# 384 unused bytes in front of the split weights' buffers of a decoder trunk

## The chip, the cores and the metric

The kernel runs on one NeuronCore of a Trainium2 chip, in float32 and float32r. The metric is the device time of one execution in microseconds (us). TensorE multiplies, ScalarE and VectorE work on elements, GpSimd does a few small operations, and SyncE (SP) issues the weight loads. On-chip memory has 128 partitions; an offset in this text is a byte offset within a partition.

## The reference, cut to what matters

256 tokens of width 2048 go through a feed-forward block, a token mixer and a second feed-forward block:

```python
def _swiglu(h, w_gu, w_down):
    gate, up = jnp.split(h @ w_gu, 2, axis=-1)
    return (jax.nn.silu(gate) * up) @ w_down
...
        x = x + 0.5 * _swiglu(_rmsnorm(x, ffn1_norm[l]), ffn1_w_gu[l], ffn1_w_down[l])
        x = x + _token_mixing(_rmsnorm(x, mix_norm[l]), w_in[l], qk_gain[l], sinks[l], cmp_pos[l], cmp_w1[l],
                              cmp_w2[l], w_branch_a[l], w_branch_b[l], w_branch_c[l], w_out[l])
        x = x + 0.5 * _swiglu(_rmsnorm(x, ffn2_norm[l]), ffn2_w_gu[l], ffn2_w_down[l])
```

The mixer is one wide input projection, three kinds of attention over it, a gated product per branch and an output projection. All weights together are 401 MB, and each is used once, so most of the work is multiplying 256 tokens with a stream of weights.

## The kernel before

**The weight stream.** Every large product goes through `add_chunk` (lines 148 to 179): an output of 256 tokens by at most 512 columns in two PSUM banks, one for each block of 128 tokens (`tb`). The weights come in loads of up to 4 x 128 rows into three buffers `raw`, issued in order by SyncE (line 103). Each load is cut into units of two slices of 128 rows, and each unit is split into two float32r parts: ScalarE copies `raw` to `hi` (line 111), and VectorE takes the rest to `lo` (line 112). There are four buffers `hi` and four `lo`, used in turn; `stream` (lines 127 to 144) splits three to four units ahead of the one that is multiplied.

**The matmuls.** The activations are split in the same way, part 0 and part 1, and are transposed, with features on the partitions. For each slice of 128 rows and each token block there are three matmuls that add up in one bank:

```python
                    PE.matmul(o, lhs(kt, 0, tb), hi[:, k], start=kt == 0, stop=False)
                    PE.matmul(o, lhs(kt, 0, tb), lo[:, k], start=False, stop=False)
                    PE.matmul(o, lhs(kt, 1, tb), hi[:, k], start=False, stop=kt == nkt - 1)
```

The first argument after the output is the stationary operand, a 128 x 128 slice of the activations that an LDWEIGHTS instruction (PEld in the profile) puts into the array. The second is the moving operand, a slice of `hi` or `lo` with up to 512 columns. These are lines 162, 163 and 164. The stationary tile depends on the stage:
- `xT`, the normalised input, in both gate-up products and in the mixer's input projection. The projection has chunks of 384, 420 and 512 columns.
- `ffn1_midt` and `ffn2_midt`, the gated hidden values, in the down products (ffn_midt in the profile);
- `oT`, the attention outputs, in the branch products, and `mT`, their gated sum, in the output projection.

**Other work of TensorE.** Transposes against `ident` of the input (line 219), of the hidden values (line 269), of queries, keys and probabilities (lines 479, 718), the float32 attention products (lines 750 to 859), and the hidden layer of the key compression (line 627), which also takes `hi` and `lo` as moving operands, with 256 columns, and slices of `Xs` with 66 columns as stationary ones. The order on each engine is the order in which the program is written: there is no scheduler.

**Where the tiles lie.** Tiles of the pool `per` stand behind one another in the order of their allocation, each rounded up to 32 bytes:

```python
    x_sb = per.tile([128, 2, D], F32, name="x_sb")
    xT = per.tile([128, KT, 2, T], F32R, name="xT")
    raws = [per.tile([128, LOAD_KT * 512], F32, name=f"raw{i}") for i in range(RAW_BUFS)]
    his = [per.tile([128, SPLIT_KT * 512], F32R, name=f"hi{i}") for i in range(SPLIT_BUFS)]
    los = [per.tile([128, SPLIT_KT * 512], F32R, name=f"lo{i}") for i in range(SPLIT_BUFS)]
    ident = per.tile([128, 128], F32, name="ident")
```

The stages' pools follow behind `per`; those that are opened with `side="right"` grow from the other end. In the built program the offsets modulo 512 bytes are:

| Tiles | modulo 512 before |
|---|---|
| `x_sb`, `xT`, `raw`, `hi`, `lo`, `ident` | 128 |
| `ffn1_midt`, `ffn2_midt`, `oT`, `mT`, and the rows that line 269 transposes (`m`) | 0 |
| `Xs` (right side) | 64; its slices step by 264 bytes |
| `pt` | 192 |

A stationary slice takes 512 bytes of a partition and a slice of `hi` or `lo` with 512 columns 2048 bytes, so every slice of these tiles begins where its tile does, modulo 512. In a chunk of 420 columns the second slice of a unit begins 1680 bytes behind the first, which is 272 modulo 512.

Of the kernel before, what the change touches and what calls it, by code (L numbers as in the profile page):

```python
# [9 lines left out]
F32 = mybir.dt.float32  # L10
# [6 lines left out]
T, D, FF = 256, 2048, 5632  # L17
# [15 lines left out]
class Ring:  # L33
    """Buffers handed out and given back in emission order."""

# [11 lines left out]
def hybrid_trunk_kernel(ctx, tc, x, ffn1_norm, ffn1_w_gu, ffn1_w_down, mix_norm, w_in, qk_gain, sinks, cmp_pos,  # L47
# [13 lines left out]
    xT = per.tile([128, KT, 2, T], F32R, name="xT")  # L61
    raws = [per.tile([128, LOAD_KT * 512], F32, name=f"raw{i}") for i in range(RAW_BUFS)]
    his = [per.tile([128, SPLIT_KT * 512], F32R, name=f"hi{i}") for i in range(SPLIT_BUFS)]
    los = [per.tile([128, SPLIT_KT * 512], F32R, name=f"lo{i}") for i in range(SPLIT_BUFS)]
# [9 lines left out]

# [1 line left out]
    chains = []  # L76
# [15 lines left out]
    loads, subs = [], []  # L92

    def add_load(src, nk, width, parts):
        """src: [128, nk, width] in DRAM; parts: [(k0, nk, mm, before, after)]"""
        li = len(loads)
        loads.append((src, nk, width))
        for k0, n, mm, before, after in parts:
            subs.append((li, k0, n, width, mm, before, after))
# [5 lines left out]
    def emit_split(si, k=None):  # L105
        """split of a unit, or of its k-th slice of 128 rows"""
        li, k0, n, width, *_ = subs[si]
        c = slice(0, n * width) if k is None else slice(k * width, (k + 1) * width)
        raw = raws[li % RAW_BUFS][:, k0 * width:(k0 + n) * width][:, c]
        hi, lo = his[si % SPLIT_BUFS][:, c], los[si % SPLIT_BUFS][:, c]  # L110
        ACT.activation(hi, raw, AF.Copy)  # L111
        DVE.tensor_tensor(lo, raw, hi.bitcast(F32), op=OP.subtract)  # L112
# [35 lines left out]
    def add_chunk(w, rows0, nkt, c0, width, lhs, evac, before=None, between=()):  # L148
        """out[tok, c0:c0+width] = lhs^T @ w[rows0:rows0+128*nkt, c0:c0+width]; lhs(kt, part, tb) -> [128, 128]."""
        bank = main[2 * (chunk_no[0] % 2):][:2]  # L150
        chunk_no[0] += 1
        wv = w[rows0:rows0 + 128 * nkt, c0:c0 + width].rearrange("(k p) c -> p k c", p=128)

        def mm_of(kt0, n):
            def mm(hi, lo):
                ks = [(k, tb) for k in range(n) for tb in range(2)]
                if kt0 + n == nkt:
                    ks.sort(key=lambda a: a[1])
                for k, tb in ks:
                    kt = kt0 + k  # L160
                    o = bank[tb][:, :width]
# [3 lines that stand above are left out]
            return mm  # L165

        step = SPLIT_KT if not loads else LOAD_KT
        for l0 in range(0, nkt, step):
            ln = min(step, nkt - l0)
            parts = []  # L170
            for s0 in range(0, ln, SPLIT_KT):
                sn = min(SPLIT_KT, ln - s0)
                last = l0 + s0 + sn == nkt
                first = l0 + s0 == 0
                parts.append((s0, sn, mm_of(l0 + s0, sn), before if first else None,
                              (lambda: evac(bank)) if last else None))
            add_load(wv[:, l0:l0 + ln], ln, width, parts)
            for args in between[l0 // step:l0 // step + 1]:
                add_load(*args)
# [14 lines left out]

# [1 line left out]
    def x_squares(j):  # L196
# [9 lines left out]
    def x_prep(norm, j):  # L206
        """The norm's share of columns 512j.., and their transposed two-part copy with the gain."""
        g0 = GAIN_ROW[norm]
# [25 lines left out]

# [1 line left out]
    def add_ffn(norm, w_gu, w_down, done):  # L236
# [68 lines left out]

# [1 line left out]
    tabs = {}  # L307
# [8 lines left out]
    def row_cols(r0, r1, c0):  # L316
        """rows [0, r1) as columns, of which [r0, r1) are kept from column c0 on"""
        b = banks.take()
        PE.transpose(b[:, :r1], rows[:r1, :], ident[:r1, :r1])
        DVE.tensor_copy(cols[:, c0:c0 + r1 - r0], b[:, r0:r1])  # L320
        banks.give(b)
# [7 lines left out]

# [1 line left out]
    def build_tables():  # L331
        """Negated key distances, far below zero where a key is masked; constants of the heads' slopes."""
        p = tab_pool
# [63 lines left out]
    def add_mix(done):  # L397
# [36 lines left out]

        # per-head norms, transposes of queries and keys
        def raw_of(bank, width):
# [5 lines left out]
        def normed(bank, qr, c0, nh, const):  # L442
            """heads in qr[:, :, c0:c0+64nh]; bank is free to be written"""
            w = 64 * nh
# [24 lines left out]
        def transposed(jobs, finish):  # L469
            """jobs: (source of tb, evac); two jobs share a bank"""  # L470
            for a in range(0, len(jobs), 2):
# [21 lines left out]
        def q_evac(name, p0, h0, const):  # L493
            """six query heads h0.. to the pairs p0.."""
            def f(bank):
# [30 lines left out]
        def both_halves(dst, src, gain):  # L526
            """dst(g)[0:64] = dst(g)[64:128] = src[64g:64g+64] * gain"""
            for g in range(2):
# [25 lines left out]
        def ckv1_evac(bank):  # L554
            """k_cmp, v_cmp, k_slc"""
            qr = raw_of(bank, 384)
# [27 lines left out]
        def make_x(i):  # L584
            """cmp MLP input of keys (0) or values (1), two-part, on partitions (offset parity, d)"""
            X, Xs = st["X"], st["Xs"]
# [13 lines left out]
        def ckv2_evac(bank):  # L600
            """v_slc, k_win, v_win, gates"""
            for tb in range(2):
# [11 lines left out]
        def cmp_loads(i):  # L614
            """hidden layer of the cmp MLP: two loads, to be set between a chunk's"""
            wv = cmp_w1[0, i].rearrange("(k p) c -> p k c", p=128)
# [74 lines left out]

        # attention
        att = {"S": True, "O": True, "obs": {}}
# [15 lines left out]
        def apply_p(sb, blocks, pv):  # L709
            """blocks: (column of sb, keys); transposes them, then pv(pt, block index)"""  # L710
            while not (banks.free and att["O"] and st["pt"].free):
# [166 lines left out]
        def launcher():  # L878
            """starts attention units at a steady pace"""
            for name, marks, group in units:  # L880
# [15 lines left out]

        # gates, branch products, output projection
        def open_gates():
# [121 lines left out]

# [1 line left out]
    x2 = x[0].rearrange("(t p) d -> p t d", p=128)  # L1022
# [47 lines left out]
    g = gens[0]  # L1070
# [50 lines left out]
```

## Time and profile before

| What | Value |
|---|---|
| median of 3 runs | 2246.64 us (2246.13 to 2247.63) |
| span of the profiled execution | 2244.8 us |
| TensorE busy | 2229.0 us, 99% of the span, 10417 matmuls |
| LDWEIGHTS busy | 1861.9 us, 83% |
| VectorE, ScalarE, GpSimd busy | 54%, 45%, 3% |
| read from HBM | 401.03 MB, 180 GB/s |

The span is one execution under the profiler, from its first to its last instruction; the times are of executions without it. A matmul's duration in a row reaches past the start of the next one, since matmuls overlap in the array. What a matmul costs in a row of many is the distance in time from its start to the next one's start, called a step below.

### The profile page before, as it was taken

The numbers are of one execution on the slowest core, as the hardware profiler recorded it, in microseconds if no ns is written. First come the engines' busy times: TensorE is split into PE (matmuls) and PEld (weight loads), VectorE is DVE, ScalarE is ACT, GpSimd is POOL, SyncE is SP. The second block draws the span as 40 slices with busy tenths as digits, with TensorE's granted clock in tenths as the row PEclk, the third lists the DMA queues.
The fourth block names the chain that finished last, engine by engine and source line by source line (L and its number), as shares of the span: only waits on it lengthen the run. The fifth ranks groups of instructions, "written<-read, shape, count | busy, mean of one in ns | idle before, by whom it ended". The sixth has DMA issues, their size and how long they took to land.

```text
span 2244.8 us, 26058 instructions
## 1 busy us (share of the span) xinstructions
PE 2229.0 (99%) x10417; PEld 1861.9 (83%) x10417; DVE 1210.3 (54%) x1618; ACT 1019.4 (45%) x1368; POOL 67.1 (3%) x83
## 2 busy tenths in 40 slices
PE   8999999999999999999999999999999999999999
PEld 7888888888888999998888888788888888888887
DVE  5755544455555576666555554555555544555553
ACT  5444433444444565555555444454444433444432
POOL 0000000000000121000001110100000000000000
PEclk9999999999999999999999999999999999999999
DMA  7555555555555564333345555555555555555553
GB/s 247 187 188 191 192 184 188 196 193 187 188 187 183 169 214 139 120 120 132 131 151 176 201 182 176 190 180 188 191 193 187 190 189 191 189 188 188 189 205 131
DMA packets 212626, 404.82 MB, mean 180 GB/s; under 512 B 7368, under 2 KB 36632, under 8 KB 212504
## 3 DMA queue, kind: packets, MB, share of 16 engines
q1 hardware_dynamic: 211696, 402.98, 52.9%
q8 instruction: 81, 1.33, 0.2%
q14 instruction: 41, 0.34, 0.0%
q10 hardware_dynamic: 808, 0.17, 0.0%
HBM read 401.03 MB, written 2.10 MB: 180 GB/s over the span
## 4 chain that ended last, share of the span: by engine, by line
PE 97%; DVE 1%; DMA 1%; POOL 0%; ACT 0%; issue 0%; SPq 0%; POOLq 0%; ACTq 0%
PE main L162 31%; PE main L164 30%; PE main L163 30%; PE misc L269 1%; PE misc L718 1%; PE misc L859 1%; PE misc L831 1%; POOL mg L958 0%; DVE lo L112 0%; PE misc L219 0%; PE misc L750 0%; PE misc L856 0%; ACT hi L111 0%; PE misc L832 0%; PE misc L769 0%
## 5 line engine op out<-in xcount | busy, mean ns | idle before, releaser
L112 DVE TENSOR_TENSOR lo<-raw,hi 128x1024 fp32r<-128x1024 f32 (+3 forms) x785 | 938.3, 1198 | 878.3 <-ACT hi L111 873.8
L111 ACT ACTIVATE hi<-raw 128x1024 fp32r<-128x1024 f32 (+3 forms) x785 | 808.1, 1032 | 922.4 <-PE main L164 906.1
L162 PE MATMUL main<-hi,xT 128*128 128x512 f32 (+1 forms) x2176 | 839.6, 386 | 3.1 <-ACT hi L111 3.1
L164 PE MATMUL main<-hi,xT 128*128 128x512 f32 (+1 forms) x2176 | 828.5, 381 | 0.0
L163 PE MATMUL main<-lo,xT 128*128 128x512 f32 (+1 forms) x2176 | 828.1, 381 | 0.1
L162 PEld LDWEIGHTS main<-hi,xT 128*128 128x128 f32 x2176 | 409.7, 188 | 81.7 <-issue 6.6
L164 PEld LDWEIGHTS main<-hi,xT 128*128 128x128 f32 x2176 | 409.0, 188 | 70.8
L163 PEld LDWEIGHTS main<-lo,xT 128*128 128x128 f32 x2176 | 409.3, 188 | 69.4 <-DVE lo L112 0.8
L162 PE MATMUL main<-hi,ffn_midt 128*128 128x512 f32 x704 | 278.4, 395 | 0.0
L164 PE MATMUL main<-hi,ffn_midt 128*128 128x512 f32 x704 | 277.9, 395 | 0.0
L163 PE MATMUL main<-lo,ffn_midt 128*128 128x512 f32 x704 | 277.8, 395 | 0.0
L164 PEld LDWEIGHTS main<-hi,ffn_midt 128*128 128x128 f32 x704 | 132.5, 188 | 31.2
L162 PEld LDWEIGHTS main<-hi,ffn_midt 128*128 128x128 f32 x704 | 132.5, 188 | 31.1
L163 PEld LDWEIGHTS main<-lo,ffn_midt 128*128 128x128 f32 x704 | 132.5, 188 | 30.9
L162 PE MATMUL main<-hi,mT 128*128 128x512 f32 x128 | 50.9, 398 | 0.0
L164 PE MATMUL main<-hi,mT 128*128 128x512 f32 x128 | 50.5, 395 | 0.0
L163 PE MATMUL main<-lo,mT 128*128 128x512 f32 x128 | 50.5, 394 | 0.0
L725 ACT ACTIVATE pt<-misc 128x256 f32<-128x256 f32 (+2 forms) x44 | 21.1, 490 | 58.8 <-PE misc L718 58.8
L190 DVE TENSOR_TENSOR ffn_midt<-misc,ffn_midt 128x512 fp32r<-128x512 f32 x44 | 28.3, 686 | 32.7 <-ACT ffn_midt L189 32.7
L189 ACT ACTIVATE ffn_midt<-misc 128x512 fp32r<-128x512 f32 x44 | 23.9, 596 | 46.4 <-PE misc L269 46.4
L845 ACT ACTIVATE sb<-sb,nm 128x32 f32<-128x32 f32 (+2 forms) x72 | 29.0, 403 | 28.9 <-DVE nm L839 28.9
L252 ACT ACTIVATE ffn_sg<-main,rstd_ffn 128x512 f32<-128x512 f32 x44 | 30.2, 688 | 22.8 <-PE main L164 20.4
(177 smaller groups left out, 1059.6 us busy)
## 6 DMA issues: line engine op xcount, KB each, us to landing
raw<-in_ffn_w_gu_dram SPq DMA_DIRECT2D x172, 1024.0 KB, 4.9
raw<-in_ffn_w_down_dram SPq DMA_DIRECT2D x88, 1024.0 KB, 5.0
raw<-in_w_in_dram SPq DMA_DIRECT2D x48, 1024.0 KB, 4.9
raw<-in_w_in_dram SPq DMA_DIRECT2D x44, 768.0 KB, 4.3
raw<-in_w_out_dram SPq DMA_DIRECT2D x16, 1024.0 KB, 5.0
raw<-in_ffn_w_gu_dram SPq DMA_DIRECT2D x8, 512.0 KB, 6.2
raw<-in_cmp_w_dram SPq DMA_DIRECT2D x4, 1024.0 KB, 5.8
raw<-in_w_branch_b_dram SPq DMA_DIRECT2D x4, 1024.0 KB, 5.0
```

Of the source, the lines that this page charges most:

```text
L111: ACT.activation(hi, raw, AF.Copy)
L112: DVE.tensor_tensor(lo, raw, hi.bitcast(F32), op=OP.subtract)
L162: PE.matmul(o, lhs(kt, 0, tb), hi[:, k], start=kt == 0, stop=False)
L163: PE.matmul(o, lhs(kt, 0, tb), lo[:, k], start=False, stop=False)
L164: PE.matmul(o, lhs(kt, 1, tb), hi[:, k], start=False, stop=kt == nkt - 1)
L189: ACT.activation(dst_hi, src, AF.Copy)
L190: DVE.tensor_tensor(dst_lo, src, dst_hi.bitcast(F32), op=OP.subtract)
L252: ACT.activation(st["sg"][tb], bank[tb], AF.Sigmoid, scale=r)
L269: PE.transpose(bv[:, k, tb * 128:(tb + 1) * 128], m[tb][:, c0:c0 + 128], ident)
L718: PE.transpose(place[i][:n], sb[:, c0:c0 + n], ident)
L831: PE.matmul(S0[:, :32 + nk], q, st["KC"][g][head_rows(h), :32 + nk], start=True, stop=True)
L845: ACT.activation(s, s, AF.Exp, bias=nm[:, 0, i:i + 1], scale=-1.0, accum_out=nm[:, 1, i:i + 1])
```

## The change

A tile of 96 float32 values per partition, 384 bytes, is allocated between `raw` and `hi`; nothing reads or writes it. `hi`, `lo` and every tile behind them on that side stand 384 bytes further: `hi` and `lo` come to 0 modulo 512, `ident` as well, and `ffn1_midt`, `ffn2_midt`, `oT`, `mT` and `m` to 384. `x_sb`, `xT`, `raw` and the tiles on the right side stay where they were.

```diff
@@ -60,6 +60,7 @@
     x_sb = per.tile([128, 2, D], F32, name="x_sb")
     xT = per.tile([128, KT, 2, T], F32R, name="xT")
     raws = [per.tile([128, LOAD_KT * 512], F32, name=f"raw{i}") for i in range(RAW_BUFS)]
+    per.tile([128, 96], F32, name="split_shift")
     his = [per.tile([128, SPLIT_KT * 512], F32R, name=f"hi{i}") for i in range(SPLIT_BUFS)]
     los = [per.tile([128, SPLIT_KT * 512], F32R, name=f"lo{i}") for i in range(SPLIT_BUFS)]
     ident = per.tile([128, 128], F32, name="ident")
```

The rest of the diff only empties comment lines, so that lines behind 62 have a number higher by one. On every engine the instructions and the waits in front of them stand in the same order as before, 13,242 rows in all; no instruction is added, removed or moved.

## Rows read from the trace of the kernel before

**Rows 1.** The page: span, granted clock by slices, the chain's shares by line.

```profile
span 2244.8 us, 26058 instructions
...
PEclk9999999999999999999999999999999999999999
...
PE main L162 31%; PE main L164 30%; PE main L163 30%; PE misc L269 1%; PE misc L718 1%; PE misc L859 1%; PE misc L831 1%; POOL mg L958 0%; DVE lo L112 0%; PE misc L219 0%; PE misc L750 0%; PE misc L856 0%; ACT hi L111 0%; PE misc L832 0%; PE misc L769 0%
```

**Rows 2.** Waits: who waited for whom, us in total, times, longest.

```profile
ACT hi L111 <- PE main L164: 906.1, 564, 1.9
```

**Rows 3.** Groups by shape, TensorE: count, busy us, mean ns, idle before.

```profile
L163 PE MATMUL main<-lo,xT 128*128 128x512 f32 x1792 | 698.7, 390 | 0.0
...
L163 PE MATMUL main<-lo,ffn_midt 128*128 128x512 f32 x704 | 277.8, 395 | 0.0
...
L163 PE MATMUL main<-lo,xT 128*128 128x384 f32 x352 | 118.1, 336 | 0.1
...
L163 PE MATMUL main<-lo,mT 128*128 128x512 f32 x128 | 50.5, 394 | 0.0
...
L163 PE MATMUL main<-lo,oT 128*128 128x512 f32 x96 | 37.9, 395 | 0.0
...
L163 PE MATMUL main<-lo,xT 128*128 128x420 f32 x32 | 11.3, 354 | 0.0
```

**Rows 4.** Timeline, gate-up product on xT: start us, us, engine, line, operands.

```profile
199.80 0.39 PE L164 MATMUL main<-hi,xT 128*128 128x512 f32 x1
200.03 0.39 PE L162 MATMUL main<-hi,xT 128*128 128x512 f32 x1
200.03 0.19 PEld L163 LDWEIGHTS main<-lo,xT 128*128 128x128 f32 x1
...
236.97 0.39 PE L163 MATMUL main<-lo,xT 128*128 128x512 f32 x1
```

**Rows 5.** Timeline, TensorE, down product of the second feed-forward.

```profile
2139.67 0.39 PE L162 MATMUL main<-hi,ffn_midt 128*128 128x512 f32 x1
...
2178.94 0.40 PE L163 MATMUL main<-lo,ffn_midt 128*128 128x512 f32 x1
```

**Rows 6.** Timeline, TensorE, down product of the first feed-forward.

```profile
299.78 0.39 PE L163 MATMUL main<-lo,ffn_midt 128*128 128x512 f32 x1
...
339.91 0.39 PE L164 MATMUL main<-hi,ffn_midt 128*128 128x512 f32 x1
```

**Rows 7.** Timeline, TensorE, input projection, a chunk of 384 columns.

```profile
756.75 0.33 PE L163 MATMUL main<-lo,xT 128*128 128x384 f32 x1
...
767.85 0.33 PE L164 MATMUL main<-hi,xT 128*128 128x384 f32 x1
```

**Rows 8.** Timeline, TensorE, hidden layer of the key compression, in two places.

```profile
792.88 0.28 PE L627 MATMUL misc<-hi,Xs 128*66 128x256 f32 x1
...
794.66 0.28 PE L627 MATMUL misc<-lo,Xs 128*66 128x256 f32 x1
...
824.80 0.28 PE L627 MATMUL misc<-hi,Xs 128*66 128x256 f32 x1
824.91 0.28 PE L627 MATMUL misc<-lo,Xs 128*66 128x256 f32 x1
```

**Rows 9.** Timeline, TensorE, where the next weight load is of another tile.

```profile
1063.70 0.39 PE L164 MATMUL main<-hi,xT 128*128 128x512 f32 x1
1063.93 0.44 PE L769 MATMUL misc<-VA,pt 128*128 128x64 f32 x3
...
1207.69 0.40 PE L162 MATMUL main<-hi,oT 128*128 128x512 f32 x1
1207.93 0.40 PE L163 MATMUL main<-lo,oT 128*128 128x512 f32 x1
```

**Rows 10.** Timeline, TensorE, the chunk of 420 columns.

```profile
774.06 0.35 PE L162 MATMUL main<-hi,xT 128*128 128x420 f32 x1
...
777.72 0.35 PE L163 MATMUL main<-lo,xT 128*128 128x420 f32 x1
```

## The prediction

> **What bounds the kernel now.** First the page: a span of 2244.8 us, the granted clock at 9 tenths or more in all forty slices, and a chain of which lines 162 to 164 on TensorE are 91% [rows 1]. Then the waits: ScalarE's split stands 906.1 us waiting for TensorE to give buffers back [rows 2]. So nothing feeds TensorE too late, and the time is the sum over its matmuls of the step from one matmul's start to the next one's start. An edit counts only if it changes that step.
>
> Then the matmuls by shape [rows 3]. With the same 128x512 moving operand (hi or lo), line 163's mean duration is 390 ns where the stationary operand is xT, but 395, 394 and 395 where it is ffn_midt, mT and oT. The timeline turns this into steps. From the start at 199.80 to that at 236.97 us are 164 steps on xT: 37.17 us, 226.65 ns each [rows 4]. On ffn_midt, 169 steps from 2139.67 to 2178.94 us: 39.27 us, 232.37 ns each [rows 5]; in the first feed-forward, 172 steps in 40.13 us, 233.3 ns [rows 6]. On xT with 384 columns, 64 steps in 11.10 us: 173.4 ns [rows 7]. The 128 columns between the two widths on xT cost 53.2 ns, which is one column per cycle at the granted 2.4 GHz; so 512 columns are 213.3 ns, and each step carries something on top: 13.3 ns at 512 and 13.4 ns at 384 columns on xT, 19.1 to 20.0 ns on the others.
>
> What differs between these cases? Instruction, shape, type and clock are the same. In the built program xT, hi and lo all begin at 128 modulo 512 bytes, and the slices that matmuls read keep that (a stationary slice is 512 bytes of a partition, a moving slice of 512 columns 2048). ffn_midt, mT and oT begin at 0. I call **distance** the moving operand's offset minus the stationary one's, modulo 512: it is 0 on xT and 128 on the others. The stationary operand meant is the next matmul's, because its LDWEIGHTS starts with the matmul and runs beside it for 0.19 us [rows 4]. That the two reads disturb each other, depending on distance, is the reading that I go by; the rows show the difference, not its cause.
>
> **The change part by part.** It adds no instruction, and all 13,242 rows of instructions and waits stand in the same order on every engine. It moves hi and lo by 384 bytes, to 0 modulo 512, and every tile behind them on that side with them: ident, the tables, ffn_midt, mT, oT. Ahead of it, x_sb, xT and the raw buffers stay, and so do the tiles allocated from the other end (QC, KC, Xs, the gate buffers).
> - ffn_midt, mT and oT (704, 128 and 96 matmuls on each of three lines, 2784 in all): moving at 0, stationary at 384, so distance 128 as before. Cost 0, if distance is what counts.
> - xT (1792, 352 and 32 matmuls on each of three lines: 5376 with 512 columns, 1056 with 384, 96 with 420 [rows 3]): distance goes from 0 to 384. No row has this distance at full rate. I bound it by the nearest ones.
> - Transposes and float32 attention products: ident moves, so distance stays 128 at line 269 and goes from 0 to 384 at line 219. No line of them has more than 1% of the chain [rows 1], and a 2% change of one would be under 0.5 us, either way. I take 0.
> - ScalarE's and VectorE's splits: read and write the moved buffers. A few ns each would vanish in the 906.1 us of slack [rows 2].
>
> Lower bound for xT: the step stays at 226.65. The argument for a floor is that 13.3 ns stands alike at both widths, so it goes with the weight load and not with the columns, and that other distances do not go below it. The hidden-layer products on Xs load only 66 columns, at sixteen offsets (distances 0 to 64, 200 to 312 and 464 to 496). 15 steps there take 1.78 us, 118.7 ns, 12.0 above the 106.7 of 256 columns; the shortest single step in the rows is 0.11 us [rows 8]. In proportion 66 columns would carry 6.9, about that shortest step. One direct look at a negative distance: an xT matmul with the weight load of pt beside it, distance 448, steps 0.23 us, not more than usual [rows 9].
>
> Upper bound: xT pays what distance 128 pays. Where the stationary operand has changed from xT to oT under way, the first step on oT is already 0.24 us, so it sets in at once [rows 9]. The 420-column chunk pays 3.66 us over 19 steps, 192.6 ns, 17.6 above its 175 [rows 10], with distances 0 and 144 in turn: so the small cost on xT needs more than distance 0, it needs steps that fall into a regular pattern. That is why I take the upper end: the steps of rows 4 are one favourable pattern, and another distance is more likely to miss it, as 128 does, than to keep it. Which of the two 384 is nearer to, no row says: modulo 256 it would be 128 itself, going round 512 it is 128 on the other side.
>
> Sum: 512 columns: 232.37 - 226.65 = 5.7 ns if every matmul were in the pattern; by the mean durations, which hold the unsettled steps behind each break, 395 against 390, 5 ns [rows 3]. I take 5.2 ns x 5376 = 28.0 us. 384 columns: 5 ns x 1056 = 5.3 us (an estimate from the 5.7 at 512). 420 columns: 0, they pay it already. Total 33.3 us on the span: 2278.1; the measured median stands 1.8 above the span (2246.64 against 2244.8), so **2280 us**, 1.5% slower.
>
> The Trainium skill speaks against any change at all: "SBUF — State Buffer", section "Who interferes with whom", gives TensorE two independent read ports, one for the moving operand and one for LDWEIGHTS, and says that it never waits on anyone. By it the sum would be 0 and the time 2246.6. The 226.65 and 232.37 ns of rows 4 and 5 do not agree with it, as nothing but offsets differs there.
>
> **The rivals.**
> - Same. 384 keeps the regular pattern, as distance 448 does in its one step [rows 9], and 13.3 ns is the floor. Then 2246.6 us. For it: that step and the equal 13.3 at two widths. Against it: 448 is only 64 bytes from 0, and 128 bytes on the other side are enough to lose it.
> - Faster, on xT: the extra time falls below 13.3 because the two reads now miss each other. It decides for faster once the step falls under 225.9 (4.5 us over 6432 matmuls). Half of it gone is 6.7 ns x 6432 = 43 us: 2204 us; all gone, 2161. Against it: the Xs steps, none far below their share. "TensorE: Matmul & The Clock Gate" of the Trainium skill (section "Wait — 56ns, not 53.3ns?") gives 215.7 ns between warm 512-column matmuls, so that, as an estimate from that page, xT's 5376 would save 59 us; no row here shows such a step.
> - Faster, on the others: absolute offsets count, not distance, and the 2784 matmuls with stationary 384 and moving 0 fall into the good pattern while xT keeps its own: 5.7 x 2784 = 15.9 us, 2231. Against it: moving lay at 128 in both groups before, so only the stationary offset would have to do it.
> - Slower than forecast: xT pays the worst of the Xs steps, 12.0 x 128 / 66 = 23.3 ns, 10 above now: 64 us, 2311.
>
> **How the numbers follow.** Forecast 0.48, same 0.32, faster on xT 0.08, faster on the others 0.08, much slower 0.04. The forecast's own range runs from 4 ns on 512 columns alone, should the pattern be a mixed one (21.5 us: 2268), to 233.3 ns as in rows 6 with 7 ns on 384 columns (35.7 + 7.4 = 43 us: 2290), and 6 us for breaks that settle later: 2296. The same-case needs down to 2240 (run scatter of 1.5 us, and up to 5 us if the 233.3 ns pattern of the first feed-forward gives way to the 232.37 one or better). 2240 to 2296 holds 0.80. A change under about 0.2% (4.5 us) cannot be told from none here: faster 0.16, same 0.33, slower 0.51.
>
> **What would show it.** In the changed kernel's groups by shape, 512 columns on xT rise from 390 to about 395 ns and its steps from 226.65 to about 232 to 233, while ffn_midt, mT and oT keep 394 to 395, LDWEIGHTS keep 0.19 us, and ScalarE's wait for TensorE grows with the span. xT at 389 to 390 means the same-case; ffn_midt at 390 means absolute offsets count; xT at 395 with ffn_midt changed as well means that distance is the wrong variable. Any new wait of TensorE would upset the whole argument.

## The result and the profile after

The changed kernel takes **2274.71 us** (median; 2272.96 to 2276.29) against 2246.39 us for the kernel before on the same chip: a ratio of 1.0126, with an interval of 1.0111 to 1.014. It is 1.3% slower, within the predicted range and 5 us below the predicted 2280.

The page of the changed kernel, beside [rows 1] (lines from 62 on have a number higher by one, so 162 to 164 are now 163 to 165):

```profile
span 2274.5 us, 26058 instructions
...
PEclk9999999999999999999999999999999999999999
...
PE main L163 30%; PE main L164 30%; PE main L165 30%; PE misc L270 1%; PE misc L719 1%; PE misc L860 1%; PE misc L832 1%; DVE lo L113 1%; ACT hi L112 1%; DMA raw<-in_cmp_w_dram 1%; POOL mg L959 0%; PE misc L220 0%; PE misc L751 0%; PE misc L857 0%; PE misc L833 0%
```

The span has grown by 29.7 us, the clock is the same, and the chain is still the three matmul lines. The waits of the changed kernel show no new wait of TensorE. ScalarE waits 932.9 us for it, 26.8 us more than in [rows 2]:

```profile
ACT hi L112 <- PE main L165: 932.9, 566, 2.2
```

The groups by shape of the changed kernel, beside [rows 3] (count, busy us, mean ns, idle before), show where TensorE became slower:

```profile
L164 PE MATMUL main<-lo,xT 128*128 128x512 f32 x1792 | 707.9, 395 | 0.0
...
L164 PE MATMUL main<-lo,ffn_midt 128*128 128x512 f32 x704 | 277.8, 395 | 0.0
...
L164 PE MATMUL main<-lo,xT 128*128 128x384 f32 x352 | 119.0, 338 | 0.0
...
L164 PE MATMUL main<-lo,mT 128*128 128x512 f32 x128 | 50.5, 395 | 0.0
...
L164 PE MATMUL main<-lo,oT 128*128 128x512 f32 x96 | 37.9, 395 | 0.0
...
L164 PE MATMUL main<-lo,xT 128*128 128x420 f32 x32 | 11.3, 353 | 0.0
```

With 512 columns, xT went from 390 to 395 ns, where the other three tiles already were and still are. With 384 columns it went from 336 to 338, and with 420 it stayed. The timeline of the changed kernel (start us, us, engine, line, operands) gives the steps, in the place of [rows 4], in the second feed-forward as in [rows 5], and on 384 columns as in [rows 7]:

```profile
199.79 0.39 PE L165 MATMUL main<-hi,xT 128*128 128x512 f32 x1
...
237.44 0.39 PE L165 MATMUL main<-hi,xT 128*128 128x512 f32 x1
```

```profile
2167.80 0.39 PE L165 MATMUL main<-hi,ffn_midt 128*128 128x512 f32 x1
...
2207.77 0.39 PE L163 MATMUL main<-hi,ffn_midt 128*128 128x512 f32 x1
```

```profile
767.70 0.34 PE L164 MATMUL main<-lo,xT 128*128 128x384 f32 x1
...
777.91 0.34 PE L165 MATMUL main<-hi,xT 128*128 128x384 f32 x1
```

On xT 162 steps take 37.65 us, 232.4 ns each, against 226.65 before. On ffn_midt 172 steps take 39.97 us, again 232.4 ns. On 384 columns 58 steps take 10.21 us, 176.0 ns against 173.4. Both 512-column stretches repeat, to within 1 ns, the same seven steps of 241, 232, 231, 232, 228, 230 and 233 ns.

The steps of every group, added up from the starts of all matmuls in the two traces, with the breaks between chunks:

| Stationary tile, columns | matmuls | before, us | after, us | difference |
|---|---|---|---|---|
| xT, 512 | 5376 | 1228.90 | 1257.13 | +28.24 |
| xT, 384 | 1056 | 191.80 | 194.01 | +2.20 |
| xT, 420 | 96 | 18.65 | 18.52 | -0.14 |
| ffn1_midt, 512 | 1056 | 246.35 | 245.79 | -0.56 |
| ffn2_midt, mT, oT, 512 | 1727 | 402.18 | 402.25 | +0.07 |
| all else | 1105 | 150.14 | 150.04 | -0.11 |

The differences add up to 29.7 us, the growth of the span.

### The profile page after: what moved, and what is told of

It is laid out like the page before. It is cut to its first block, busy times and chain, and to the rows that moved or that the text cites. A ratio compares the mean times of both kernels' runs of the same rounds, so it can differ in the third digit from the quotient of the medians.

```text
span 2274.5 us, 26058 instructions
## 1 busy us (share of the span) xinstructions
PE 2257.9 (99%) x10417; PEld 1866.9 (82%) x10417; DVE 1209.8 (53%) x1618; ACT 1019.4 (45%) x1368; POOL 67.6 (3%) x83
## 4 chain that ended last, share of the span: by engine, by line
PE 95%; issue 1%; DMA 1%; DVE 1%; ACT 1%; POOL 1%; SPq 0%; ACTq 0%; POOLq 0%; DVEq 0%
PE main L163 30%; PE main L164 30%; PE main L165 30%; PE misc L270 1%; PE misc L719 1%; PE misc L860 1%; PE misc L832 1%; DVE lo L113 1%; ACT hi L112 1%; DMA raw<-in_cmp_w_dram 1%; POOL mg L959 0%; PE misc L220 0%; PE misc L751 0%; PE misc L857 0%; PE misc L833 0%
## 5 line engine op out<-in xcount | busy, mean ns | idle before, releaser
L112 ACT ACTIVATE hi<-raw 128x1024 fp32r<-128x1024 f32 (+3 forms) x785 | 808.1, 1032 | 946.7 <-PE main L165 932.9
L163 PE MATMUL main<-hi,xT 128*128 128x512 f32 (+1 forms) x2176 | 849.6, 390 | 2.9 <-ACT hi L112 2.9
L164 PE MATMUL main<-lo,xT 128*128 128x512 f32 (+1 forms) x2176 | 838.2, 385 | 0.0
L165 PE MATMUL main<-hi,xT 128*128 128x512 f32 (+1 forms) x2176 | 837.9, 385 | 0.0
```

## The experiments

The theory is that of the prediction: a matmul's step depends on the distance between its moving operand and the stationary operands, and on nothing else that the change moves. The rivals are that the tiles' own offsets count, that the period is not 512 bytes, and that only the slice loaded beside a matmul counts. A **settled step** below is the mean over a stretch behind its first 14 steps. Where a kernel has more lines, the three matmul lines have higher numbers.

### All distances at 0

```diff
     los = [per.tile([128, SPLIT_KT * 512], F32R, name=f"lo{i}") for i in range(SPLIT_BUFS)]
+    per.tile([128, 32], F32, name="pad_post")
     ident = per.tile([128, 128], F32, name="ident")
```

> 128 unused bytes behind lo instead of 384 in front of hi. hi, lo and xT stay at 128 modulo 512, and ffn_midt, oT and mT come to 128 as well, so the distance from stationary to moving operand is 0 for every product of the weight stream. Theory (distance sets the step): the 2784 matmuls on ffn_midt, oT and mT fall from 232.4 to 226.7 ns, 15.9 us less than the kernel before: about 2230.5 us. Rival (the stages differ by something else, such as the data or the neighbouring work): they stay at 232.4 ns, 2246 us.

Measured: 2230.85 us (2230.09 to 2231.62), a ratio of 0.9932 (0.9917 to 0.9947). Groups by shape of this kernel, and its timeline in the second feed-forward:

```profile
L164 PE MATMUL main<-lo,ffn_midt 128*128 128x512 f32 x704 | 273.9, 389 | 0.0
...
L164 PE MATMUL main<-lo,mT 128*128 128x512 f32 x128 | 49.8, 389 | 0.0
L164 PE MATMUL main<-lo,oT 128*128 128x512 f32 x96 | 37.4, 389 | 0.0
```

```profile
2139.76 0.39 PE L165 MATMUL main<-hi,ffn_midt 128*128 128x512 f32 x1
...
2179.88 0.39 PE L165 MATMUL main<-hi,ffn_midt 128*128 128x512 f32 x1
```

The three tiles fall to 389 ns, and 177 steps take 40.12 us: 226.67 ns, as on xT. The same variable that made the changed kernel slower makes this one faster, on the other tiles. By the sum over the starts ffn1_midt, ffn2_midt, mT and oT together lose 16.1 us and xT with 512 columns 0.2. This version beats both kernels.

### The tiles' own offsets, with the distances as before

```diff
     x_sb = per.tile([128, 2, D], F32, name="x_sb")
+    per.tile([128, 32], F32, name="pad_xT")
     xT = per.tile([128, KT, 2, T], F32R, name="xT")
```

> 128 unused bytes in front of xT: xT, hi and lo all move together, from 128 to 256 modulo 512, ffn_midt, oT and mT from 0 to 128. Distances stay 0 and 128. Theory (distance alone counts): no change, 2246 us, xT at 226.7 and the others at 232.4 ns. Rival (the stationary operand's own offset counts, 128 being good): xT at 256 loses 5.7 ns x 6432 and the others at 128 gain 5.7 ns x 2784: about 2266 us.

Measured: 2246.13 us, a ratio of 0.9999 (0.9989 to 1.0008). The timeline of this kernel on xT and in the first feed-forward:

```profile
199.74 0.39 PE L163 MATMUL main<-hi,xT 128*128 128x512 f32 x1
...
237.37 0.39 PE L164 MATMUL main<-lo,xT 128*128 128x512 f32 x1
```

```profile
300.22 0.39 PE L164 MATMUL main<-lo,ffn_midt 128*128 128x512 f32 x1
...
332.88 0.39 PE L163 MATMUL main<-hi,ffn_midt 128*128 128x512 f32 x1
```

166 steps on xT take 37.63 us (226.7 ns) and 140 on ffn1_midt 32.66 us (233.3 ns), as in [rows 4, 6]. All of these tiles moved by 128 bytes together and nothing changed, so for a shift of 128 bytes the offsets themselves don't count. Other common shifts were not run.

### Other distances

```diff
+    per.tile([128, 64], F32, name="pad_hi")
     his = [per.tile([128, SPLIT_KT * 512], F32R, name=f"hi{i}") for i in range(SPLIT_BUFS)]
...
+            p.tile([128, 96 if norm == "ffn1" else 48], F32, name="pad_mid")
             st["mid"] = p.tile([128, 24, 2, T], F32R, name=f"{norm}_midt")
```

> 256 unused bytes in front of hi instead of 384, and pads in front of the stationary tiles: distance 256 on xT and ffn1_midt, 448 on ffn2_midt, 384 on oT, 320 on mT. If distance counts modulo 256, xT and ffn1_midt step 226.7 ns as at distance 0, oT 232.4 as at 128, and the time is 2240 to 2248 us. If it counts modulo 512, 256 is a case of its own, most likely in the unsettled pattern: xT about 232 ns and the time about 2275 us. 448 and 320 are not predicted (226.7 for 448 by its one step before).

Measured: 2239.52 us (2237.8 to 2239.85), a ratio of 0.997 (0.9957 to 0.9982). The timeline of this kernel, on xT at distance 256 and in the second feed-forward at 448:

```profile
199.62 0.39 PE L163 MATMUL main<-hi,xT 128*128 128x512 f32 x1
...
237.47 0.40 PE L165 MATMUL main<-hi,xT 128*128 128x512 f32 x1
```

```profile
2161.80 0.39 PE L164 MATMUL main<-lo,ffn_midt 128*128 128x512 f32 x1
...
2189.80 0.39 PE L164 MATMUL main<-lo,ffn_midt 128*128 128x512 f32 x1
```

At 256, 167 steps take 37.85 us: 226.65 ns, the same as at 0. At 448, 120 steps take 28.00 us: 233.3 ns. So the period is 256 bytes, not 512, and 64 bytes to the other side (448) already lose the good step.

```diff
+    per.tile([128, 32], F32, name="pad_hi")
     his = [per.tile([128, SPLIT_KT * 512], F32R, name=f"hi{i}") for i in range(SPLIT_BUFS)]
...
+            p.tile([128, 16 if norm == "ffn1" else 8], F32, name="pad_mid")
             st["mid"] = p.tile([128, 24, 2, T], F32R, name=f"{norm}_midt")
```

> 128 unused bytes in front of hi instead of 384: distance 128 on xT; pads make it 64 on ffn1_midt, 96 on ffn2_midt, 32 on oT and 480 on mT. Theory: xT takes exactly what ffn_midt has at 128 in the kernel before, 232.4 ns, and its share of the time is that of the changed kernel (about 28 us more than before). Rival (the changed kernel's loss belongs to its absolute offsets, hi at 0): xT at 226.7 ns. The four others show the curve between 0 and 128: somewhere between 226.7 and 233 ns.

Measured: 2274.55 us (2274.11 to 2275.67), a ratio of 1.0127 (1.0112 to 1.0142), the same as that of the changed kernel. The timeline of this kernel, on xT at distance 128 and in the first feed-forward at 64:

```profile
199.74 0.39 PE L163 MATMUL main<-hi,xT 128*128 128x512 f32 x1
...
237.38 0.40 PE L163 MATMUL main<-hi,xT 128*128 128x512 f32 x1
```

```profile
300.24 0.39 PE L165 MATMUL main<-hi,ffn_midt 128*128 128x512 f32 x1
...
332.97 0.39 PE L164 MATMUL main<-lo,ffn_midt 128*128 128x512 f32 x1
```

162 steps on xT take 37.64 us, 232.3 ns: 128 costs what 384 costs. At 64, 143 steps take 32.73 us: 228.9 ns.

### Small distances, and a shorter weight load

The kernel with all distances 0 again, with the hidden values 16 or 8 bytes beside their place, and with half of each stationary slice in the output projection, whose other half is left out:

```diff
+            k = 60 if norm == "ffn1" else 62
+            midt = p.tile([128, 48 * T + 64], F32R, name=f"{norm}_midt")
+            st["mid"] = midt[:, k:k + 48 * T].rearrange("p (a b t) -> p a b t", b=2, t=T)
...
+            add_chunk(w_out[0], 0, KT, 512 * j, 512, part_of("mT", st), out_evac(j), cut=2)
```

> The kernel of e1_all_zero with finer distances: 16 bytes (modulo 256) on ffn1_midt, 8 on ffn2_midt, 160 on oT, xT stays at 0. In the output projection (mT, distance 0) the stationary operand is cut to the first 64 of each 128 tokens, so that the weight load is half as long; half of that product is left out. If the extra time at distance 0 belongs to the weight load, the steps on mT fall from 226.7 to 213.3 + 13.3 / 2 = 220.0 ns; if it is a fixed cost of each matmul, they stay at 226.7. For 16 and 8: if even small distances lose the regular pattern, 229 to 233 ns, as at 32; if only whole multiples of some line count, 226.7. Below 226.7 would mean that 0 is not the best distance; I give that one in ten.

Measured: 2240.57 us in one run. The timeline of this kernel in the second feed-forward, at distance 8; then, from its groups by shape, the weight loads of mT (count, busy us, mean ns), and its timeline on mT:

```profile
2151.68 0.40 PE L165 MATMUL main<-lo,ffn_midt 128*128 128x512 f32 x1
...
2184.81 0.40 PE L166 MATMUL main<-hi,ffn_midt 128*128 128x512 f32 x1
```

```profile
L164 PEld LDWEIGHTS main<-hi,mT 128*64 128x64 f32 x128 | 17.2, 134 | 11.6
```

```profile
1439.65 0.39 PE L166 MATMUL main<-hi,mT 128*64 128x512 f32 x1
...
1451.83 0.40 PE L165 MATMUL main<-lo,mT 128*64 128x512 f32 x1
```

At 8 bytes 142 steps take 33.13 us, 233.3 ns: two float32 values are enough to lose all of it. The half load takes 134 ns where a whole one takes 188, but 53 steps take 12.18 us, 229.8 ns, which is more than the 226.7 of whole loads. Both forecasts for mT, 220.0 and 226.7 ns, fell. That speaks against the reason that the prediction gave for its floor, that the 13.3 ns above the columns go with the weight load.

The settled steps of 512 columns over all these kernels, by distance modulo 256:

| distance | settled step, ns | seen on |
|---|---|---|
| 0 | 226.67 | all five tiles |
| 8 | 233.33 | ffn2_midt |
| 16 | 228.33 in three of five stretches, 226.67 in two; mean 228.0 | ffn1_midt |
| 32 | 233.32 | oT |
| 64 | 228.89 | ffn1_midt, mT |
| 96 | 233.33 | ffn2_midt |
| 128 | 232.3 to 232.5, or 233.3 | all five tiles |
| 160 | 234.29 | oT |
| 192 | 233.33 | ffn2_midt |
| 224 | 233.31 | mT |

No distance goes below 226.67, and the curve is not smooth. Nor does the distance alone fix the step: on xT at 128, 20 of the 25 long stretches settle at 232.4 ns and five at 233.3, in one and the same kernel (the last one under "Other distances"; a long stretch has 54 steps or more). At 0 every long stretch settles at 226.67.

### Three lengths of weight load

All distances at 0 and fewer tokens in the stationary slices of three products, whose other tokens are left out:

```diff
+                    o = bank[tb][:cut, :width]
+                    PE.matmul(o, lhs(kt, 0, tb)[:, :cut], hi[:, k], start=kt == 0, stop=False)
```

> All stationary and moving operands of the large products at distance 0, with the stationary operand cut to its first tokens: 32 of each 128 in the output projection (mT), 96 in the branch products (oT), 64 in the down product of the second feed-forward; the other tokens of these products are left out. Theory 'the extra over 213.3 ns goes with the length of the weight load' (13.3 ns for 128 tokens): steps of 216.7 ns on mT, 223.3 on oT, 220.0 on the second feed-forward. Rival 'the extra comes from the pattern that the starts settle into, which a shorter load does not improve': 226 to 234 ns in all three, as the 64-token load on mT gave 229.9. xT and the first feed-forward keep 226.7. Time by the theory about 2214 us, by the rival 2231 to 2240 us.

Measured: 2236.44 us in one run. From this kernel's groups by shape, the weight loads of mT; then its timeline in the second feed-forward (64 tokens) and on mT (32 tokens):

```profile
L164 PEld LDWEIGHTS main<-lo,mT 128*32 128x32 f32 x128 | 14.0, 109 | 15.1
```

```profile
2139.80 0.40 PE L164 MATMUL main<-lo,ffn_midt 128*64 128x512 f32 x1
...
2174.99 0.39 PE L164 MATMUL main<-lo,ffn_midt 128*64 128x512 f32 x1
```

```profile
1439.64 0.39 PE L163 MATMUL main<-hi,mT 128*32 128x512 f32 x1
...
1451.92 0.40 PE L165 MATMUL main<-hi,mT 128*32 128x512 f32 x1
```

With 64 tokens 153 steps take 35.19 us, 230.0 ns; with 32 tokens 53 steps take 12.28 us, 231.7 ns; with 96 tokens the settled step is 230.0. The load itself gets shorter (188, 134 and 109 ns at 128, 64 and 32 tokens), and the step gets longer by 3 to 5 ns. The extra time does not go with the length of the load. That it comes from how load and matmul fall into step is a reading that no run isolates; of the four lengths, 128 tokens at distance 0 have the shortest step.

### Whose stationary slice counts

In the kernel before, a matmul's own stationary operand and the one that is loaded beside it (the next matmul's) lie at the same distance. Three kernels part them. In the first, part 1 of xT stands 128 bytes further than part 0, and `lo` 128 further than `hi`, so that on xT the next slice is at distance 0 on all three lines and the own one at 0, 128 and 128:

```diff
-    xT = per.tile([128, KT, 2, T], F32R, name="xT")
+    xT0 = per.tile([128, KT, T], F32R, name="xT")
+    per.tile([128, 32], F32, name="pad_x1")
+    xT1 = per.tile([128, KT, T], F32R, name="xTb")
...
+    per.tile([128, 32], F32, name="pad_lo")
     los = [per.tile([128, SPLIT_KT * 512], F32R, name=f"lo{i}") for i in range(SPLIT_BUFS)]
```

> xT is two tiles, part 1 128 bytes (modulo 256) off part 0, and lo is 128 off hi. On xT the moving operand then has distance 0 to the next matmul's stationary operand in all three lines, but 0, 128, 128 to its own (lines 166, 167, 168 there). Theory (the next weight load counts, as it runs beside the matmul): xT keeps 226.7 ns. Rival (its own stationary operand counts): xT loses the pattern, about 229 to 233 ns. On ffn_midt, oT and mT lo is at 128 and hi at 0 to both: steps between 226.7 and 233 ns, no forecast.

Measured: 2270.31 us in one run, with a settled step of 231.1 ns on xT. On ffn_midt, oT and mT, where only the `lo` line is at distance 128, it is 233.3 to 233.4 ns. The timeline of this kernel on mT, 52 steps in 12.13 us:

```profile
1439.66 0.39 PE L168 MATMUL main<-hi,mT 128*128 128x512 f32 x1
...
1451.79 0.40 PE L166 MATMUL main<-hi,mT 128*128 128x512 f32 x1
```

The next slice at distance 0 was not enough, so the prediction's "the stationary operand meant is the next matmul's" falls. There is more in this run: on mT the two `hi` lines, whose own and next slices are both at 0, have means of 235.8 and 230.0 ns, and the `lo` line between them 233.9. One line off its place disturbs all three.

In the second, only part 1 of xT is moved, and all else is at distance 0:

```diff
+    xT0 = per.tile([128, KT, T], F32R, name="xT")
+    per.tile([128, 32], F32, name="pad_x1")
+    xT1 = per.tile([128, KT, T], F32R, name="xTb")
...
+    per.tile([128, 32], F32, name="pad_post")
     ident = per.tile([128, 128], F32, name="ident")
```

> Part 1 of xT 128 bytes off part 0, lo and hi together, ffn_midt, oT and mT at 0. On xT the distance to the next stationary operand is 0, 128, 0 in lines 166, 167, 168, to its own 0, 0, 128. Theory (the next one counts): line 167's step is longer than 226.7 ns, as its weight load is the one at 128; the step of 168, whose own operand is at 128, is not the long one. Rival: line 168's step is the long one. The others stay at 226.7 ns as in e1_all_zero.

Measured: 2254.43 us in one run. The timeline of this kernel on xT:

```profile
199.72 0.39 PE L167 MATMUL main<-lo,xT 128*128 128x512 f32 x1
...
237.40 0.40 PE L168 MATMUL main<-hi,xTb 128*128 128x512 f32 x1
```

163 steps take 37.68 us, 231.2 ns, while the other tiles keep 226.67. By line, the first (own 0, next 0) has a mean of 227.0 ns, the second (own 0, next 128) 232.5, the third (own 128, next 0) 233.9. By the theory the third was not to be long; the second and the third both are.

In the third, `lo` stands 128 bytes further than `hi`, and in the second feed-forward line 164 takes a copy of part 0 that stands at `lo`'s offset, so that there every own slice is at 0 and the next one at 128, 128 and 0:

```diff
+    per.tile([128, 32], F32, name="pad_lo")
     los = [per.tile([128, SPLIT_KT * 512], F32R, name=f"lo{i}") for i in range(SPLIT_BUFS)]
...
-                    PE.matmul(o, lhs(kt, 0, tb), lo[:, k], start=False, stop=False)
+                    PE.matmul(o, lhs(kt, 2, tb), lo[:, k], start=False, stop=False)
...
+                if norm == "ffn2":
+                    POOL.tensor_copy(st["midc"][:, k0:k0 + 2], st["mid"][:, k0:k0 + 2, 0])
```

> The lo buffers stand 128 bytes further than hi (modulo 256: hi at 128, lo at 0 relative to 128, so lo is at distance 128 from hi), and in the second feed-forward GpSimd keeps a second copy of part 0 of the hidden values at lo's offset, which line 163 uses as its stationary operand. So there every matmul has its own stationary operand at distance 0, but the stationary operand that is loaded beside it (the next matmul's) is at distance 128, 128 and 0 over the three lines. On xT, oT, mT and the first feed-forward hi is at distance 0 from the stationary operand and lo at 128, as a control: steps of about 231 to 233.5 ns. Theory 'a matmul's own stationary operand counts': 226.7 ns on the second feed-forward's down product. Rival 'all three offsets, hi, lo and the stationary ones, must agree': 229 to 233.5 ns there. Time by the first about 2274 us, by the second about 2277 us.

Measured: 2270.15 us in one run. The timeline of this kernel in the second feed-forward:

```profile
2191.76 0.39 PE L164 MATMUL main<-lo,ffn_midc 128*128 128x512 f32 x1
...
2224.81 0.39 PE L163 MATMUL main<-hi,ffn_midt 128*128 128x512 f32 x1
```

143 steps take 33.05 us, 231.1 ns; the own slice at distance 0 was not enough either. In every long stretch that reached 226.67 ns with whole loads, but two at 16 bytes, `hi`, `lo` and all stationary slices lay at the same offset modulo 256. With any of the three kinds moved by 128 it was 231.1 to 233.4 ns. Which of these it is, the distances don't say: in the first feed-forward `hi` is at 0 and `lo` at 128 both here and in the first of the three kernels, and its settled step is 231.1 ns here and 233.4 there. On xT, with these distances too, 15 of this kernel's 25 long stretches settle at 231.1 and ten at 233.4, and its time lies 4 and 7 us under the two forecasts. What chooses between the two patterns is open.

### How the cost goes with the columns

The changed kernel paid 2.7 ns on 384 columns, half of what the prediction took. Two kernels give four widths, one at distance 128 (the kernel before) and one at 0 (the kernel with all distances 0); the other columns are left out:

```diff
+                    c = min(width, cols)
+                    o = bank[tb][:, :c]
+                    PE.matmul(o, lhs(kt, 0, tb), hi[:, k, :c], start=kt == 0, stop=False)
```

> The kernel before with the distances as they were (0 on xT, 128 on the others), and fewer columns of the moving operand in the products at distance 128: 448 of 512 in the first feed-forward's down product, 384 in the second's, 480 in the output projection, 320 in the branch products; the other columns of these products are left out. Reading 'what distance 128 costs goes with the columns' (5.7 ns at 512): above columns plus 13.3 ns it costs 5.3 at 480 (steps of 218.7 ns), 5.0 at 448 (205.0), 4.3 at 384 (177.6), 3.6 at 320 (150.2). Reading 'each width settles into its own pattern': 2.7 at 384 (176.0 ns), as on xT in the changed kernel, though with another tile and distance 128 in place of 384, and no straight line through the others. Time about 2130 us if the loads keep up, later if the stream of weights becomes the bound in a stage.

> The same four widths (448, 384, 480 and 320 of 512 columns, the other columns left out) in the kernel with all distances at 0. If what stands above one column per cycle is the same 13.3 ns at every width, as at 512 and 384: steps of 213.3 ns at 480, 200.0 at 448, 173.3 at 384, 146.7 at 320. If a width besides 512 and 384 has no pattern as good: some ns more there. Time about 2118 us if the loads keep up.

Measured: 2149.12 us and 2143.75 us in one run each. The timeline of the first of them, in the second feed-forward (384 columns) and the first (448):

```profile
2071.69 0.34 PE L164 MATMUL main<-lo,ffn_midt 128*128 128x384 f32 x1
...
2095.98 0.34 PE L164 MATMUL main<-lo,ffn_midt 128*128 128x384 f32 x1
```

```profile
300.34 0.36 PE L165 MATMUL main<-hi,ffn_midt 128*128 128x448 f32 x1
...
332.98 0.36 PE L163 MATMUL main<-hi,ffn_midt 128*128 128x448 f32 x1
```

And the timeline of the second, with all distances 0, on 448 columns:

```profile
300.18 0.36 PE L165 MATMUL main<-lo,ffn_midt 128*128 128x448 f32 x1
...
332.81 0.36 PE L164 MATMUL main<-hi,ffn_midt 128*128 128x448 f32 x1
```

The 138 steps at 384 columns take 24.29 us (176.0 ns); at 448 columns 160 steps take 32.64 us at distance 128 (204.0 ns), and 161 take 32.63 us at 0 (202.7). All settled steps, in ns:

| columns | one per cycle at 2.4 GHz | distance 0 | distance 128 | difference |
|---|---|---|---|---|
| 512 | 213.3 | 226.67 | 232.4 or 233.3 | 5.7 or 6.7 |
| 480 | 200.0 | 216.67 | 220.00 (217.81 in one stretch of four) | 3.3 (1.1) |
| 448 | 186.7 | 202.65 | 203.98 | 1.3 |
| 384 | 160.0 | 173.33 | 175.99 | 2.7 |
| 320 | 133.3 | 146.67 | 146.70 | 0 |

The cost of distance 128 is no rate per column. At 384 it is 2.7 ns on ffn2_midt too, so 2.7 belongs to this width and not to xT or to distance 384. The other forecast fell in part: what stands above one column per cycle at distance 0 is 13.3 ns at 512, 384 and 320 columns, but 16.0 at 448 and 16.7 at 480. The times came out 19 and 26 us later than forecast. In the second kernel the steps at 448 and 480 columns, longer than forecast, are 4 us of that. Most of the rest lies in the branch products and just behind them, where TensorE, with its shorter products, waits longer for GpSimd's gated sum `mg` (waits of the kernel with all distances 0, then of the second kernel):

```profile
PE misc L938 <- POOL mg L959: 4.8, 4, 1.4
...
PE misc L939 <- POOL mg L960: 17.0, 8, 4.4
```

That is 12.2 us more. In or just behind these waits, which come two in a row (4.4 and 1.7 us at first), the granted clock falls from 2.4 to 1.2 GHz four times, for 20.5 us in all in either kernel. By the steps of the three lines in these stretches against the settled ones, the second kernel loses some 7 us there (an estimate). The timeline of the first kernel shows such a stretch on mT, at 480 columns and distance 128:

```profile
1381.95 0.60 PE L163 MATMUL main<-hi,mT 128*128 128x480 f32 x1
...
1384.75 0.60 PE L164 MATMUL main<-lo,mT 128*128 128x480 f32 x1
```

Seven steps take 2.80 us, 400.0 ns each, which is one column per cycle at 1.2 GHz with nothing on top. The settled steps in the table are from stretches at 2.4 GHz without a break.

## Why the prediction was right

- **What bounds the kernel.** Right. The sum over TensorE's steps explains the growth of the span, 29.7 us, with no new wait, and ScalarE's wait for TensorE grew with it.
- **xT with 512 columns.** Right in sign and size: 5.2 ns x 5376 = 28.0 us was forecast, and 28.24 us came, 5.25 ns a matmul. The choice of the upper end rested on the argument that another distance rather misses the good pattern than keeps it. Of the nine distances other than 0 that ran, all miss it, by 1.3 to 7.6 ns (at 16 bytes two stretches of five kept it). Modulo 256, 384 is 128 itself, which the prediction named as one of two readings: it is the right one.
- **xT with 384 columns.** The mis-sized term: 5 ns x 1056 = 5.3 us was an estimate from 512 columns, and 2.20 us came. The settled step rose by 2.7 ns; taking a cost from one width to another was the error, as the five widths show. With 2.7 in its place the forecast would have been 2277.5.
- **420 columns, ffn_midt, mT, oT, transposes and float32 products.** Forecast 0, measured -0.14, -0.49 and -0.11 us. Most of the -0.49 is in the first feed-forward, where a stretch changed from the 233.3 ns pattern to the 232.4 one; the prediction had allowed for that in its range. The second slice of a 420-column unit begins 144 bytes further modulo 512, as the prediction has it; the 272 in the section on the tiles is a slip.
- **The span against the time.** The median stood 1.8 us above the span before and 0.2 after (2274.71 against 2274.5). The profiled execution was itself the slowest of the four (2276.29 us, 1.8 above its span), so this is scatter between executions. Of the 5.3 us by which the forecast was high, 3.1 are the 384 columns, 1.6 this scatter, and the rest the small terms.
- **The reasons.** "Distance counts, not the offset" stands for what was run: moving these tiles together by 128 bytes changed nothing, and one tile of 128 bytes between `lo` and what follows gave 0.7%. But away from 0 equal distances can settle at different steps. Three steps of the reasoning fell; the sum did not rest on them, since its price for xT came from the steps and mean durations on xT and ffn_midt. The period is 256 bytes, not 512. The stationary operand meant is not the next matmul's alone, nor the own alone. And the floor had the wrong reason: a shorter weight load does not lower the 13.3 ns, which is not the same at all widths. The floor itself held: no settled step with 512 columns was below 226.67 ns.
- **The rivals.** "Same" would have needed 384 to keep the pattern; 448, on whose one step it leaned [rows 9], costs 233.3 ns once steps have settled, so that single step, the last one before another product, told nothing. "Faster on the others by absolute offsets" fell with the kernel that moved all tiles. "Faster on xT" fell with the curve over ten distances. By the Trainium skill's "SBUF — State Buffer", section "Who interferes with whom", TensorE's two read ports are independent and it waits on no one, which would have made the sum 0. The 28.24 us don't agree with a sum of 0 for these float32r matmuls; whether the ports are the reason, no run shows. The Trainium skill's "TensorE: Matmul & The Clock Gate", section "Wait — 56ns, not 53.3ns?", has 215.7 ns between warm 512-column matmuls. No settled stretch of 512 columns here is below 226.67.

What stays open is the cause below the step. That the reads of moving and stationary operands get in each other's way fits the runs, and so does any other mechanism that depends on both offsets modulo 256 bytes; no run here observes the reads themselves.

## What to carry to other kernels

Where TensorE is the bound and steps of equal shape differ by a few per cent between stages, compare the on-chip offsets of moving and stationary operands: in this kernel, 128 unused bytes that bring all of them to the same offset modulo 256 (128 here; others than 0 and 128 were not run) were worth 0.7% over the kernel before and 2% over the changed one. Lay out such tiles on purpose, since any tile allocated ahead of them can change it. And take such a cost from a settled stretch of the same width: neither one step nor another width gives it.

## What was not expected of the hardware

- A displacement of 8 bytes costs 6.7 ns a matmul of 512 columns, as much as 192; one of 16 costs 1.3 in the mean and one of 64 2.2 ns.
- With 320 columns distance 128 costs nothing (146.7 ns at both). Nor does it with 480 columns while the granted clock is 1.2 GHz: 400.0 ns, one column per cycle.
- Weight loads of 32, 64 or 96 tokens make a 512-column step 3 to 5 ns longer than one of 128 tokens at distance 0, though the load takes 109 ns instead of 188.
- Settled steps repeat to within 1 ns: three steps of 226, 227 and 227 ns at distance 0, seven steps from 228 to 241 ns in one of the patterns at 128. At a distance other than 0 one and the same layout can settle into either of two patterns (231.1 or 233.4 ns, 232.4 or 233.3).
